# Two feed-forward layers of a streaming encoder: 16 of 22 up-projection tiles as seven block products instead of eight

## The chip, the cores and the metric

The kernel runs on one core of a Trainium2 chip, as one launch. The metric is the time of one execution on the device in microseconds. Before the change it is 1991.15 us (median of three runs, 1991.13 to 1991.19).

A core has engines that run side by side, each through its own list of instructions in order: TensorE (PE; weight loads are shown apart as PEld), VectorE (DVE), ScalarE (ACT), GpSimd (POOL) and SyncE (SP), which issues the DMAs here. TensorE reads its operands from SBUF, the on-chip memory of 128 partitions, and adds up in PSUM, which has eight banks of 512 float32 numbers per partition.

## The reference

One layer of an encoder over 512 prompt tokens and 8 x 16 sample tokens, 640 tokens together, with width 1024. It is a feed-forward part (FFN 1), a mixer of three branches (windowed attention, the gated recurrence HGRN2, and a gated linear recurrence, RG-LRU), and a second feed-forward part (FFN 2). The change is in the two feed-forward parts:

```python
D_MODEL = 1024
D_FF = 2816

def rms_norm(x, g):
    xf = x.astype(jnp.float32)
    y = xf * lax.rsqrt(jnp.mean(xf * xf, axis=-1, keepdims=True) + EPS)
    return y.astype(x.dtype) * g

def swiglu(h, w_up, w_down):
    gate, val = jnp.split(h @ w_up, 2, axis=-1)
    return (jax.nn.silu(gate) * val) @ w_down

def layer_forward(x, p, lb, cache, win_rows):
    x = x + 0.5 * swiglu(rms_norm(x, p['norm_ffn1']), p['w_ffn1_up'], p['w_ffn1_down'])
    m, st = mixer(rms_norm(x, p['norm_mix']), p, lb, cache, win_rows)
    x = x + m
    x = x + 0.5 * swiglu(rms_norm(x, p['norm_ffn2']), p['w_ffn2_up'], p['w_ffn2_down'])
    return x, st
```

All arrays are float32.

## The kernel before

**Layout.** Activations are held transposed: a block of 128 channels lies on the 128 partitions, and the 640 tokens (`T`) run along it. The 1024 channels are eight such blocks. The residual `X` has eight blocks of 640. A weight tile is 1024 x 128: eight blocks of 128 x 128 for one block of 128 outputs.

**High and low parts.** TensorE takes operands of a reduced float32 form (`F32R`). To keep the precision, every operand is split into a high part (a copy into that form) and a low part (the difference), and each product is three matmuls: high x high, high x low and low x high. `RA` and `RB` hold an activation each: eight blocks of high parts and eight of low parts.

**A projection** (`proj`, L648 to 660) loads one weight tile of 512 KB by DMA into one of three buffers `wr`, makes its high part `wh` (L654, on ScalarE or VectorE) and low part `wl` (L655, VectorE), and issues 8 blocks x 3 parts x 2 token halves = 48 matmuls of 320 columns each, into a PSUM buffer `pp` of two banks, one half of the tokens in each. There are two `pp` buffers. `scaled` (L662) moves the result out of PSUM and multiplies it by the norm's factor `RS` of each token; the gain of the norm is in `RA` or `RB` already.

**A feed-forward part** (`ffn`, L677 to 691) goes through 22 tiles of the hidden width 2816 in groups of 8, 8 and 6. For a tile, it projects the gate, applies silu (ScalarE), projects the value, multiplies the two, and splits the product into its parts in `H` (`parts`, L672). After a group it projects the group down (`w_down`) for all eight blocks of outputs and adds half of that to the residual (L689). In the last group, `done(m)` follows for each block: in FFN 1 the next norm's sums and a copy of the block to DRAM, in FFN 2 the transposes and stores of the result.

**Order of the work.** The order is made when the kernel is built. Each operation goes to a planner (`Sched`) with its reads, its writes, a duration by a small formula for its engine, and a priority. The planner lists the operations of each engine in the order in which, by these durations, they could start; among those that could start within 0.04 us it takes the one with the lowest priority number. The priority is the number of the projection (`S.item`), in program order. Three kinds of work are asked for earlier, by a lag in projections: the weight load (4), the high part (2) and the low part (1.5). Buffers with one name (a tag) are handed out in program order, and a tag that lies over the space of another waits until all of that one's buffers have been handed out and those in the way are free. On the chip each engine then runs its list in order, with semaphores for the waits.

**Space.** One array `AR` of 25600 numbers per partition holds all scratch; `arena` lays tags over it, so that FFN 1, attention, LRU, HGRN and FFN 2 use the same space one after another.

Matmuls of all kinds are issued at L394, transposes at L402; VectorE's additions and products stand at L334, its combined operation with a scalar at L348; ScalarE's functions at L358, copies at L364; DMAs at L379. The profile names lines, and most of these are the helpers' lines, so tile names (`pp`, `wr`, `wh`, `RA`) tell the groups apart.

Of the kernel before, what the change touches and what calls it, by code (L numbers as in the profile page):

```python
# [8 lines left out]
F32 = mybir.dt.float32  # L9
# [85 lines left out]
class Slot:  # L95
    __slots__ = ("ap", "lo", "hi", "free", "owner", "before")

    def __init__(self, ap, lo=None, hi=None):
        self.ap, self.lo, self.hi, self.free, self.owner, self.before = ap, lo, hi, 0.0, None, []

# [32 lines left out]
class Sched:  # L133
# [12 lines left out]
    def tag(self, name, slots, psum=False):  # L146
        for s in slots:
            for u in self.tags.values():
                v = [v for v in u.slots if s.lo is not None and v.lo is not None and v.lo < s.hi and s.lo < v.hi]
# [86 lines left out]
    def run(self):  # L236
# [13 lines left out]
        for _ in range(len(self.ops)):  # L250
# [38 lines left out]
            for b, s in zip([b for b in o.news if b.slot is None], slots):  # L289
                b.slot, b.ap, s.owner = s, s.ap, b  # L290
# [20 lines left out]
def trunk_kernel(ctx: ExitStack, tc: tile.TileContext, A: dict, O: list):  # L311
# [107 lines left out]
    DER = fixed("DER", [P, 40])  # L419
# [4 lines left out]
    NAR = 100 * 256  # L424
# [29 lines left out]
    arena(M0, [("X2", M0, 1)])
    arena(2 * M0, [("sq2", T, 1), ("acc2", T, 2), ("nh2", T, 3), ("fA2", T, 2), ("fB2", T, 2), ("yo", T, 3)])
# [134 lines left out]
    def pv(ps):  # L590
        return ps.v.r("p (a b) -> p a b", a=2)[:, :, :HT]
# [56 lines left out]
    def proj(w, r0, nk, c0, R):  # L648
# [607 lines left out]
```

## Time and profile before

| | |
|---|---|
| median of three runs | 1991.15 us |
| the profiled execution | 1991.13 us, of it 1989.3 us are the span of the profile |
| TensorE | 15086 matmuls |
| weight loads of the up-projections | 88 of 512 KB |
| VectorE, ScalarE instructions | 1922, 978 |
| granted TensorE clock, mean | 0.998 of full speed |

The time of the execution is a little more than the span: the span runs from the first to the last recorded instruction. A row of a group gives the line, the engine, the operation, the output and the inputs with their sizes, and the count; behind the bar come the busy time in us, the mean duration of one in ns, and the time that the engine stood idle just before them, with the engine and line that ended most of it. A row of the timeline gives start and duration in us; a bracket behind it is the idle time before. In the chain of waits, each piece is what held up the next.

### The profile page before, as it was taken

To read this page: it belongs to the slowest core of one execution; us is meant where nothing else is said; L and a number is where in the kernel's file an instruction comes from. 1 tells how busy PE (TensorE), PEld (TensorE's weight loads), DVE (VectorE), ACT (ScalarE), POOL (GpSimd) and SP (SyncE) were. 2 spreads that over 40 slices of the span, in tenths; PEclk is the share of its full clock that TensorE was granted. 3 is DMA by queue.
4 is the path that set the end of the run, shared out by engine and by line. 5 is a ranking of instruction groups with operands and counts; after the bars stand their busy time and mean duration, and the time that the engine had idled before them with its cause. 6 is when DMAs were issued, how large, how long until landed. Compare 5 with 4: busy or idle time off the path is not lost.

```text
span 1989.3 us, 34591 instructions
## 1 busy us (share of the span) xinstructions
PE 1959.9 (99%) x15086; PEld 1915.1 (96%) x15086; DVE 1159.4 (58%) x1922; ACT 557.3 (28%) x978; POOL 31.5 (2%) x61
## 2 busy tenths in 40 slices
PE   6999999999999999999999999999999999999998
PEld 5999999999999999999999999999999999999998
DVE  4543444456677783677557788886555443444444
ACT  5110010012468850798002333334112100110000
POOL 0000000000000000020000000000000000000000
PEclk9999999999999999999999999999999999999999
DMA  4222222224412212222322222223322222222223
GB/s 128 77 75 75 75 75 74 75 67 129 121 54 59 64 49 77 75 58 78 87 77 83 77 77 81 84 77 119 85 75 75 75 75 74 75 75 74 75 64 85
DMA packets 304434, 156.85 MB, mean 79 GB/s; under 512 B 22645, under 2 KB 301782, under 8 KB 304282
## 3 DMA queue, kind: packets, MB, share of 16 engines
q1 hardware_dynamic: 304282, 154.63, 27.0%
q8 instruction: 118, 1.93, 0.4%
q14 instruction: 34, 0.28, 0.0%
HBM read 143.32 MB, written 10.63 MB: 77 GB/s over the span
## 4 chain that ended last, share of the span: by engine, by line
PE 92%; ACT 3%; DVE 2%; SPq 1%; DMA 1%; issue 1%; DVEq 0%; ACTq 0%
PE pp L394 84%; PE me L394 4%; PE ml L394 3%; ACT L358 1%; PE ml L402 1%; ACT AR L358 1%; SPq L379 1%; PE me L402 1%; DVE AR L334 1%; DMA SK<-in_attn_sinks_dram 1%; DVE AR L348 1%; DVE RB L334 0%; DVE AR L996 0%; DMA wr<-in_w_in_dram 0%; DVE wl L655 0%
## 5 line engine op out<-in xcount | busy, mean ns | idle before, releaser
L394 PE MATMUL pp<-RA,wh 128*128 128x320 f32 x5056 | 968.1, 313 | 0.3 <-DVE RA L348 0.3
L394 PEld LDWEIGHTS pp<-RA,wh 128*128 128x128 f32 x5056 | 791.6, 189 | 10.8 <-issue 7.6
L394 PE MATMUL pp<-RA,wl 128*128 128x320 f32 x2528 | 576.7, 309 | 0.0
L394 PE MATMUL pp<-RB,wh 128*128 128x320 f32 x2880 | 539.5, 309 | 0.0
L654 DVE CAST wh<-wr 128x1024 fp32r<-128x1024 f32 (+1 forms) x221 | 151.3, 685 | 600.4 <-PE pp L394 598.8
L394 PEld LDWEIGHTS pp<-RB,wh 128*128 128x128 f32 x2880 | 452.5, 188 | 0.0
L394 PEld LDWEIGHTS pp<-RA,wl 128*128 128x128 f32 x2528 | 423.8, 188 | 0.3 <-DVE wl L655 0.2
L394 PE MATMUL pp<-RB,wl 128*128 128x320 f32 x1440 | 328.3, 309 | 0.0
L655 DVE TENSOR_TENSOR wl<-wr,wh 128x1024 fp32r<-128x1024 f32 (+1 forms) x252 | 302.5, 1200 | 0.6 <-DVE AR L334 0.4
L358 ACT ACTIVATE AR<-AR 128x640 f32<-128x640 f32 (+2 forms) x216 | 147.7, 685 | 522.3 <-DVE AR L334 503.2
L394 PEld LDWEIGHTS pp<-RB,wl 128*128 128x128 f32 x1440 | 241.2, 188 | 0.3 <-DVE wl L655 0.3
L334 DVE TENSOR_TENSOR AR<-AR 128x640 f32<-128x640 f32 (+8 forms) x380 | 198.4, 545 | 38.9 <-ACT AR L358 31.2
L334 DVE TENSOR_TENSOR AR<-pp,RS 128x640 f32<-128x640 f32 x168 | 137.5, 819 | 8.5 <-PE pp L394 8.1
L358 ACT ACT_TABLE_LOAD x97 | 124.5, 1283 | 5.8 <-DVE AR L334 3.7
L364 ACT CAST RA<-AR 128x640 fp32r<-128x640 f32 x30 | 21.8, 728 | 211.9 <-DVE AR L334 205.8
L364 ACT CAST RB<-AR 128x640 fp32r<-128x640 f32 x38 | 27.6, 726 | 177.1 <-DVE AR L334 177.1
L394 PE MATMUL ml<-AR 128*128 128x128 f32 (+6 forms) x576 | 68.3, 314 | 0.0
L394 PEld LDWEIGHTS me<-AR 128*32 128x32 f32 (+2 forms) x2016 | 50.5, 118 | 14.6 <-issue 9.5
L394 PE MATMUL me<-AR 128*32 128x16 f32 (+6 forms) x2016 | 63.9, 206 | 0.0
L364 ACT COPY AR<-me 128x512 f32<-128x512 f32 (+3 forms) x72 | 26.0, 375 | 115.5 <-PE me L402 92.2
L394 PEld LDWEIGHTS ml<-AR 128*128 128x128 f32 (+2 forms) x576 | 46.9, 151 | 11.6 <-ACT AR L364 2.6
L348 DVE SCALAR_TENSOR_TENSOR AR<-AR,PRM 64x512 f32<-64x512 f32 (+6 forms) x92 | 52.0, 582 | 0.9
(111 smaller groups left out, 894.0 us busy)
## 6 DMA issues: line engine op xcount, KB each, us to landing
wr<-in_w_ffn_up_dram SPq DMA_DIRECT2D x88, 512.0 KB
wr<-in_w_in_dram SPq DMA_DIRECT2D x84, 512.0 KB
wr<-in_w_ffn_down_dram SPq DMA_DIRECT2D x32, 512.0 KB
wr<-in_w_ffn_down_dram SPq DMA_DIRECT2D x16, 384.0 KB
wr<-in_w_attn_o_dram SPq DMA_DIRECT2D x8, 512.0 KB
AR<-in_state_hgrn_dram SPq DMA_DIRECT2D x8, 512.0 KB
wr<-in_w_lru_o_dram SPq DMA_DIRECT2D x8, 512.0 KB
out_dram<-AR SPq DMA_DIRECT2D x8, 512.0 KB
```

The lines of the kernel that those rows point to most:

```text
L334: alts = [dve(out.n, lambda: nc.vector.tensor_tensor(out(), a(), b(), op=op))]
L348: return S.op([dve(out.n, lambda: nc.vector.scalar_tensor_tensor(out(), a(), ap_of(s), b(), op0=op0, op1=op1), isinstance(s, View))], [a, ...
L358: nc.scalar.activation(out(), a(), func, bias=ap_of(bias), scale=ap_of(scale), **kw)
L364: alts = [act(out.n, lambda: nc.scalar.copy(out(), a()), 0, a), dve(out.n * (1.0 if a.in_psum else 0.5), lambda: nc.vector.tensor_copy(out ...
L379: return S.op([("SP", 0.47, lambda: nc.sync.dma_start(ap_of(out), ap_of(a)))], [a], [out], dma=v.n * 4 * v.proto.shape[0], lag=lag)
L394: nc.tensor.matmul(o(), l(), m(), start=s, stop=e)
L402: nc.tensor.transpose(o(), i(), d())
L654: S.op([act(nk * P, lambda: nc.scalar.copy(h(), r())), dve(nk * P * 0.5, lambda: nc.vector.tensor_copy(h(), r()))], [r], [h], lag=2)
L655: S.op([dve(nk * P, lambda: nc.vector.tensor_tensor(l(), r(), h().bitcast(F32), op=ALU.subtract))], [r, h], [l], lag=1.5)
```

## The change

For tiles 6 to 21 of each feed-forward part, gate and value are now made together (`pair`). The 1024 channels are cut into two halves and the 640 tokens into two halves, so the normed activations are a 2 x 2 of blocks `x11`, `x12`, `x21`, `x22`, and the weights of gate and value a 2 x 2 as well (`g1`, `g2`, `u1`, `u2`). Their block product, eight products of blocks, is done with seven by Strassen's method in Winograd's form: four sums of activation blocks (`t1` to `t4`), made once per layer (`combos` and its `rest`), four sums of weight blocks (`s1` to `s4`) in each pair, and seven additions of the results. Each product is 4 blocks x 3 parts = 12 matmuls of 320 columns into one PSUM bank.

Since the sums need the same scale for each token, the activations are normed first: `combos` multiplies `X` by gain and `RS`, and `pair` has no `RS` behind it. The first six tiles stay as they were, except that their result is moved out of PSUM half by half. The groups of tiles are now 6, 8 and 8. `combos` is issued behind tile 2; `rest` behind tile 5, since it writes over the operand of the first six tiles (`R`).

`pp` becomes four buffers of one bank each for two of two, and every reader of a projection now reads two banks in two instructions. The value weights have a buffer of their own, `vr` (one), beside the three `wr`; parts of the weight sums are in `vh` and `vl` (four each). To make room, `AR` shrinks from 25600 to 13864 numbers; three regions `RX`, `RY` and `RW` beside it change between float32 and `F32R` use from phase to phase, and a phase begins only when the one before is wholly done. The scratch tags of all stages are laid out anew.

```diff
+class Region:
+    def __init__(self, name, base, n, protos, make):
+        self.name, self.base, self.n, self.protos, self.make = name, base, n, protos, make
+        self.now, self.tiles = -1, {}
+    def tile(self, phase):
+        if phase not in self.tiles:
+            assert phase > self.now
+            self.now = phase
+            self.tiles[phase] = self.make(self.name, self.n, phase)
+        assert phase == self.now
+        return self.tiles[phase]
+    def slots(self, phase, at, n, k):
+        return [Slot(self.protos[phase][:, a:a + n], self.base + a, self.base + a + n, self, phase)
+                for a in range(at, at + n * k, n) if a + n <= self.n or 1 / 0]
 
 
...
-    for name, n, w in (("pp", 2, 1024), ("me", 2, 512), ("ml", 2, 512)):
+    for name, n, w in (("pp", 4, 512), ("me", 2, 512), ("ml", 2, 512)):
...
+    def combos_tags(sfx, ry, rx, at):
+        S.tag("vx" + sfx, RW.slots(rx - 1, 0, T, 6) + of_ar(at, T, 4))
+        S.tag("vB" + sfx, RX.slots(rx, 0, 2560, 2) + RY.slots(ry, 0, 2560, 1))
+        arena(at, [("vS" + sfx, 512, 3), ("vr" + sfx, 1024, 1)])
+        in_region(RW, rx, [("vh" + sfx, 512, 4), ("vl" + sfx, 512, 4)])
...
         S.op([dve(nk * P, lambda: nc.vector.tensor_tensor(l(), r(), h().bitcast(F32), op=ALU.subtract))], [r, h], [l], lag=1.5)
-        ps = S.buf("pp")
+        ps = [S.buf("pp") for _ in range(2)]
         for k in range(nk):
-            mm([(pv(ps)[:, i, :], a[:, k, :], R[:, o + k, i * HT:(i + 1) * HT].at(o + k), k == 0 and j == 0, k == nk - 1 and j == 2)
+            mm([(ps[i][:, :HT], a[:, k, :], R[:, o + k, i * HT:(i + 1) * HT].at(o + k), k == 0 and j == 0, k == nk - 1 and j == 2)
                 for j, (a, o) in enumerate(((wh, 0), (wh, 8), (wl, 0))) for i in range(2)])
         return ps
 
     def scaled(tag, ps, late=False):
 
         b = S.buf(tag)
+        for i, (o, p) in enumerate(halves(b.v, ps)):
+            if late:
+                cp(o, p, only=("ACT", "DVE"))
+            else:
+                tt(o, p, hv(RS.v)[:, i, :], ALU.mult)
         if late:
-            cp(hv(b.v), pv(ps), only=("ACT", "DVE"))
             tt(b.v, b.v, RS.v, ALU.mult)
-        else:
-            tt(hv(b.v), pv(ps), hv(RS.v), ALU.mult)
         return b
 
...
-    def ffn(wu, wd, R, H, sfx, done):
-        for f0, nf in ((0, 8), (8, 8), (16, 6)):
+    def combos(norm, R, sfx):
+        vs = [S.buf("vx" + sfx).v for _ in range(8)]
+        for k in range(KD):
+            h, q = k // 4, (k % 4) // 2
+            for n in range(2):
+                o = vs[(h * 2 + q) * 2 + n].r("p (a b) -> p a b", a=2)[:, k % 2, :].at(k % 2)
+                stt(o, hv(xk(k))[:, n, :], prm(norm + k), hv(RS.v)[:, n, :], ALU.mult, ALU.mult)
+        def x(h, n, q):
+            return vs[(h * 2 + q) * 2 + n]
+        def put(dst, q, v):
+            hi, lo = dst(0, q), dst(1, q)
+            cp(hi, v, only=("ACT",))
+            tt(lo, v, hi.cast(F32), ALU.subtract)
+        def in_r(j):
+            return lambda part, q: R[:, 4 * j + 2 * part + q, :].at(4 * j + 2 * part + q)
+        def in_b(b):
+            return lambda part, q: b[:, (2 * part + q) * T:(2 * part + q + 1) * T].at((part, q))
+        vb = [in_b(S.buf("vB" + sfx)) for _ in range(3)]
+        ops = {"x11": in_r(0), "x21": in_r(1), "x22": in_r(2), "t1": in_r(3), "t2": vb[0], "t3": vb[1], "t4": vb[2]}
+        for q in range(2):
+            a, b = S.buf("vx" + sfx), S.buf("vx" + sfx)
+            tt(a.v, x(1, 1, q), x(0, 1, q), ALU.subtract)
+            put(ops["t3"], q, a.v)
+            tt(b.v, x(0, 1, q), x(0, 0, q), ALU.subtract)
+            tt(b.v, x(1, 1, q), b.v, ALU.subtract)
+            put(ops["t2"], q, b.v)
+            tt(b.v, x(1, 0, q), b.v, ALU.subtract)
+            put(ops["t4"], q, b.v)
+        def rest():
+            for q in range(2):
+                put(ops["x11"], q, x(0, 0, q))
+            for name, h, n in (("x21", 1, 0), ("x22", 1, 1)):
+                for q in range(2):
+                    put(ops[name], q, x(h, n, q))
+            for q in range(2):
+                tt(x(0, 1, q), x(0, 1, q), x(0, 0, q), ALU.subtract)
+                put(ops["t1"], q, x(0, 1, q))
+        return ops, rest
+    def pair(wu, f, ops, sfx):
+        S.item += 2
+        gr, ur = S.buf("wr"), S.buf("vr" + sfx)
+        U = ur.v.r("p (k f) -> p k f", k=KD)
+        for v, c0 in ((gr.v, f * P), (U, FF + f * P)):
+            dma(v, wu[:, c0:c0 + P].rearrange("(k p) f -> p k f", p=P), lag=6)
+        def sub(out, a, b, lag, op=ALU.subtract):
+            S.op([dve(out.n, lambda: nc.vector.tensor_tensor(out(), a(), b(), op=op))], [a, b], [out], lag=lag)
+        def hi(out, a, lag):
+            S.op([act(out.n, lambda: nc.scalar.copy(out(), a()))], [a], [out], lag=lag)
+        def half(b):
+            return b.v.r("p (k f) -> p k f", k=4)
+        wh, wl = S.buf("wh"), S.buf("wl")
+        hi(wh.v, gr.v, 3.0)
+        sub(wl.v, gr.v, wh.v.cast(F32), 2.9)
+        G, g1, g2, u1, u2 = {}, gr[:, 0:4, :], gr[:, 4:8, :], U[:, 0:4, :], U[:, 4:8, :]
+        s1, s2, s3, s4 = (S.buf("vS" + sfx) for _ in range(4))
+        def parts_of(name, v, lag):
+            h, l = S.buf("vh" + sfx), S.buf("vl" + sfx)
+            H, L = half(h), half(l)
+            hi(H, v, lag)
+            sub(L, v, H.cast(F32), lag - 0.1)
+            G[name] = H, L
+        sub(half(s1), u1, u2, 2.8, ALU.add)
+        sub(half(s2), half(s1), g1, 2.75)
+        parts_of("s2", half(s2), 2.7)
+        sub(half(s3), g1, u1, 2.4)
+        parts_of("s3", half(s3), 2.35)
+        parts_of("u2", u2, 2.05)
+        parts_of("s1", half(s1), 1.7)
+        sub(half(s4), g2, half(s2), 1.4)
+        parts_of("s4", half(s4), 1.35)
+        G["g1"], G["g2"] = ((wh[:, o:o + 4, :], wl[:, o:o + 4, :]) for o in (0, 4))
+        def product(w, x):
+            (H, L), B, ps = G[w], ops[x], S.buf("pp")
+            def of(part, k):
+                return B(part, k // 2).r("p (a b) -> p a b", a=2)[:, k % 2, :]
+            for q in range(2):
+                mm([(ps[:, :HT], a[:, k, :], of(part, k), k == 0 and j == 0, k == 3 and j == 2)
+                    for k in (2 * q, 2 * q + 1) for j, (a, part) in enumerate(((H, 0), (H, 1), (L, 0)))])
+            return ps[:, :HT]
+        g, u = S.buf("fA" + sfx), S.buf("fB" + sfx)
+        (g0, g1_), (u0, u1_) = ([hv(b.v)[:, i, :].at(i) for i in range(2)] for b in (g, u))
+        cp(u0, product("g1", "x11"), only=("ACT",))
+        tt(g1_, product("s2", "t2"), u0, ALU.add)
+        tt(g0, product("g2", "x21"), u0, ALU.add)
+        fn(g0, g0, AF.Silu)
+        tt(u1_, product("s3", "t3"), g1_, ALU.add)
+        tt(u0, product("u2", "t4"), u1_, ALU.add)
+        ps = product("s1", "t1")
+        tt(u1_, ps, u1_, ALU.add)
+        tt(g1_, ps, g1_, ALU.add)
+        tt(g1_, product("s4", "x22"), g1_, ALU.add)
+        fn(g1_, g1_, AF.Silu)
+        return g, u
+    def ffn(wu, wd, norm, R, H, sfx, done, aside=()):
+        ops = None
+        for f0, nf in ((0, 6), (6, 8), (14, 8)):
             for f in range(nf):
-                late = not sfx and f0 + f < 2
-                g = scaled("fA" + sfx, proj(wu, 0, KD, (f0 + f) * P, R), late)
-                fn(g.v, g.v, AF.Silu)
-                u = scaled("fB" + sfx, proj(wu, 0, KD, FF + (f0 + f) * P, R), late)
+                for at, job in aside:
+                    if at == f0 + f:
+                        job()
+                if f0:
+                    g, u = pair(wu, f0 + f, ops, sfx)
+                else:
+                    late = not sfx and f < 2
+                    g = scaled("fA" + sfx, proj(wu, 0, KD, f * P, R), late)
+                    fn(g.v, g.v, AF.Silu)
+                    u = scaled("fB" + sfx, proj(wu, 0, KD, FF + f * P, R), late)
                 tt(u.v, g.v, u.v, ALU.mult)
                 parts(H, f, u.v)
+                if f0 + f == 2:
+                    ops, rest = combos(norm, R, sfx)
+            if f0 == 0:
+                rest()
             for m in range(KD):
                 ps = proj(wd, f0 * P, nf, m * P, H)
-                x = xk(m)
-                stt(hv(x), pv(ps), 0.5, hv(x), ALU.mult, ALU.add)
-                if f0 == 16:
+                for o, p in halves(xk(m), ps):
+                    stt(o, p, 0.5, o, ALU.mult, ALU.add)
+                if f0 == 14:
                     done(m)
 
...
-    ffn(A["w_ffn1_up"][0], A["w_ffn1_down"][0], RA, RB, "", spill)
+    ffn(A["w_ffn1_up"][0], A["w_ffn1_down"][0], G1, RA, RB, "", spill)
...
-    ffn(A["w_ffn2_up"][0], A["w_ffn2_down"][0], RB, RA, "2", finish)
+    ffn(A["w_ffn2_up"][0], A["w_ffn2_down"][0], G2, RB, RA, "2", finish)
```

More of the change, by code (lines that the diff above doesn't have):

```diff
@@ L95, with __init__, place @@
 class Slot:
-    __slots__ = ("ap", "lo", "hi", "free", "owner", "before")
-    def __init__(self, ap, lo=None, hi=None):
+    __slots__ = ("ap", "lo", "hi", "free", "owner", "before", "region", "phase")
+    def __init__(self, ap, lo=None, hi=None, region=None, phase=0):
         self.ap, self.lo, self.hi, self.free, self.owner, self.before = ap, lo, hi, 0.0, None, []
+        self.region, self.phase = region, phase
+    def place(self):
+        return self.ap if self.region is None else self.region.tile(self.phase)[:, self.lo - self.region.base:self.hi - self.region.base]
+class Region:
[12 more added lines that the diff above has]
+                for a in range(at, at + n * k, n) if a + n <= self.n or 1 / 0]
 class Tag:
@@ L148, in tag @@
             for u in self.tags.values():
-                v = [v for v in u.slots if s.lo is not None and v.lo is not None and v.lo < s.hi and s.lo < v.hi]
+                v = [v for v in u.slots if s.lo is not None and v.lo is not None and (v.lo < s.hi and s.lo < v.hi or
+                     s.region is not None and v.region is s.region and v.phase < s.phase)]
                 if v:
@@ L454, in trunk_kernel, with make @@
-    arena(M0, [("X2", M0, 1)])
-    arena(2 * M0, [("sq2", T, 1), ("acc2", T, 2), ("nh2", T, 3), ("fA2", T, 2), ("fB2", T, 2), ("yo", T, 3)])
+    R_, F_ = RA.v.r("p k t -> p (k t)")(), AR
+    types = {"RX": (F32, F32R, F32, F32R), "RY": (F32R, F32, F32R), "RW": (F32, F32R, F32, F32R)}
+    def make(name, n, phase):
+        return pool.tile([P, n], types[name][phase], tag=name, name=f"{name}{phase}")
+    RX, RY, RW = (Region(name, base, n, [R_ if t is F32R else F_ for t in types[name]], make)
+                  for name, base, n in (("RX", 100000, M0), ("RY", 200000, 4 * T), ("RW", 300000, 4096)))
@@ new lines, in in_region, with of_ar @@
+    def in_region(region, phase, tags):
+        at = 0
+        for name, n, k in tags:
+            S.tag(name, region.slots(phase, at, n, k))
+            at += n * k
+    def of_ar(at, n, k):
+        assert at + n * k <= NAR
+        return [Slot(AR[:, a:a + n], a, a + n) for a in range(at, at + n * k, n)]
+    def combos_tags(sfx, ry, rx, at):
[3 more added lines that the diff above has]
+        in_region(RW, rx, [("vh" + sfx, 512, 4), ("vl" + sfx, 512, 4)])
@@ new lines, in trunk_kernel @@
+    F0 = M0 + T + 1024 + 6 * T
+    in_region(RX, 0, [("x0", 1024, 4), ("xs", 1024, 1)])
+    arena(0, [("X1", M0, 1), ("sq", T, 1), ("pst", 1024, 1), ("fA", T, 2), ("fB", T, 2), ("acc", T, 2)])
+    combos_tags("", 0, 1, F0)
+    arena(F0, [("nh", T, 3)])
+    in_region(RX, 2, [("MG", M0, 1)])
+    in_region(RY, 1, [("gx", T, 4)])
+    in_region(RW, 2, [("qb", 1024, 2), ("pw", 1024, 2)])
+    arena(0, [("ck", 512, 1), ("kc", 1024, 1), ("vc", 512, 2), ("vd", 1280, 1),
+              ("kd", T, 4), ("pT", 1792, 1), ("sS", 512, 1), ("sT", 512, 1), ("sO", 256, 1), ("qs", 256, 2), ("ms", 512, 1),
+              ("qq", T, 2), ("qt", T, 1), ("qr", T, 1), ("qu", T, 1), ("sm", 16, 4)])
@@ L456, in trunk_kernel @@
+    in_region(RW, 2, [("mgB", T, 6)])
+    A2 = M0 + 7 * T
+    arena(0, [("X2", M0, 1)])
+    arena(M0, [("sq2", T, 1), ("acc2", T, 2), ("fA2", T, 2), ("fB2", T, 2), ("nh2", T, 3)])
+    combos_tags("2", 2, 3, A2)
+    arena(A2, [("yo", T, 3)])
     dram = ctx.enter_context(tc.tile_pool(name="dram", bufs=1, space=bass.MemoryType.DRAM))
@@ L588, in hv, with halves @@
         return v.r("p (a b) -> p a b", a=2)
-    def pv(ps):
-        return ps.v.r("p (a b) -> p a b", a=2)[:, :, :HT]
+    def halves(v, ps):
+        return [(hv(v)[:, i, :], p[:, :HT]) for i, p in enumerate(ps)]
     class Norm:
@@ L718, in gate @@
         g = mg(m) if tag is None else S.buf(tag).v
-        tt(hv(g), pv(proj(W, 0, KD, col + m * P, RA)), hv(RS.v), ALU.mult)
+        for i, (o, p) in enumerate(halves(g, proj(W, 0, KD, col + m * P, RA))):
+            tt(o, p, hv(RS.v)[:, i, :], ALU.mult)
         fn(g, g, AF.Sigmoid)
@@ L725, in merge @@
             ps = proj(wo, 0, KD, m * P, RB)
-            if gates is None:
-                tt(hv(mg(m)), pv(ps), hv(mg(m)), ALU.mult)
-            else:
-                g = gates[m]
-                tt(hv(g), pv(ps), hv(g), ALU.mult)
+            g = mg(m) if gates is None else gates[m]
+            for o, p in halves(g, ps):
+                tt(o, p, o, ALU.mult)
+            if gates is not None:
                 tt(mg(m), mg(m), g, ALU.add)
@@ L1204, in trunk_kernel @@
         x = xk(m)
-        tt(hv(x), pv(ps), hv(x), ALU.add)
+        for o, p in halves(x, ps):
+            tt(o, p, o, ALU.add)
         n2.add(m)
```

26 lines of the change are left out of this document (10 added, 16 removed).

## The prediction

> **What bounds the kernel now.** I read the page's busy times first, then the chain of waits that ended last, then the stretches of the two feed-forward layers (FFN 1 and FFN 2), then single instructions there.
>
> ```profile
> span 1989.3 us, 34591 instructions
> PE 1959.9 (99%) x15086; PEld 1915.1 (96%) x15086; DVE 1159.4 (58%) x1922; ACT 557.3 (28%) x978; POOL 31.5 (2%) x61
> PE 92%; ACT 3%; DVE 2%; SPq 1%; DMA 1%; issue 1%; DVEq 0%; ACTq 0%
> ```
>
> TensorE is busy all the time and carries 92% of the chain. A busy TensorE need not be at its peak, so the chain in order of time (start, us, what) gives its pace, and the busy times by stretch show who else works there:
>
> ```profile
> 45.82 449.68 PE pp L394 x3066
> 1521.50 424.16 PE pp L394 x2892
> 1956.98 5.28 PE pp L394 x36
> ...
> core 0: us, PE busy (x) PEld busy (x) DVE busy (x) ACT busy (x) POOL busy (x), PEclk, DMA share, GB/s
> 35.00:500.00 465.00, 465.00 (x3165) 464.77 (x3165) 224.72 (x304) 52.99 (x76) 2.47 (x5) 1.00 0.28 82
> 806.00:926.00 120.00, 114.68 (x764) 111.81 (x763) 93.06 (x167) 108.12 (x134) 12.80 (x16) 1.00 0.22 65
> 1010.00:1380.00 370.00, 370.00 (x4033) 345.04 (x4032) 282.24 (x530) 121.81 (x209) 6.42 (x17) 1.00 0.27 78
> 1500.00:1975.00 475.00, 475.00 (x3248) 474.99 (x3247) 219.86 (x268) 43.35 (x61) 0.00 (x0) 1.00 0.26 75
> ```
>
> 449.68 / 3066 and 424.16 / 2892 both give 0.1467 us per matmul of 128x128 by 320 columns, in one unbroken piece each, at a granted clock of 1.00. In both layers nothing but the number of matmuls sets the time. VectorE is busy 48% (224.72 / 465), ScalarE 11%, DMA 28%. So fewer matmuls means less time, for as long as VectorE, which gets the new work, stays under TensorE's time.
>
> **The change, part by part.**
>
> *Matmuls removed.* One tile of an up-projection is now two projections (gate and value) of 8 blocks x 3 high/low parts x 2 token halves = 96 matmuls, 96 x 0.1467 = 14.08 us. As seven block products it is 7 x 4 blocks x 3 parts = 84, 12.32 us. 12 matmuls fewer in 16 tiles of 2 layers: 384 x 0.1467 = 56.3 us. The down-projections only change how 22 tiles are grouped (6, 8, 8 for 8, 8, 6): 22 x 8 x 6 matmuls either way, no difference.
>
> Could the matmuls themselves get dearer? The old code alternates two PSUM banks; a product puts 12 matmuls in a row into one. Gate matmuls of the LRU stage do three in a row into one bank, each with other weights or another operand:
>
> ```profile
> 805.54 0.31 PE L394 MATMUL me<-NH,BH 128*128 128x320 f32 x1
> 805.69 0.31 PE L394 MATMUL me<-NL,BH 128*128 128x320 f32 x1
> 805.84 0.30 PE L394 MATMUL me<-NH,BL 128*128 128x320 f32 x1
> 805.98 0.31 PE L394 MATMUL me<-NH,BH 128*128 128x320 f32 x1
> 806.12 0.31 PE L394 MATMUL me<-NL,BH 128*128 128x320 f32 x1
> 806.27 0.31 PE L394 MATMUL me<-NH,BL 128*128 128x320 f32 x1
> ```
>
> Their starts are 0.14 to 0.15 us apart, the same pace. And the page counts as many weight loads as matmuls (15086 of each), so the shared weights of two neighbours saved no load before. I take 0.1467.
>
> *VectorE's new work in a pair (gate and value of one tile).* From the diff: the low part of the gate weights (1024 elements), four sums of weight blocks and five low parts (nine of 512), seven additions that read products from PSUM (320 each), then as before the product of gate and value and its low part (640 each): 19 instructions. Groups by form (busy, mean ns | idle before), and a piece of the timeline (start, duration):
>
> ```profile
> L655 DVE TENSOR_TENSOR wl<-wr,wh 128x1024 fp32r<-128x1024 f32 x236 | 287.3, 1217 | 0.6 <-DVE AR L334 0.4
> L334 DVE TENSOR_TENSOR AR<-pp,RS 128x640 f32<-128x640 f32 x168 | 137.5, 819 | 8.5 <-PE pp L394 8.1
> L334 DVE TENSOR_TENSOR AR<-me,AR 128x512 f32<-128x512 f32 x8 | 5.5, 690 | 0.8 <-PE me L394 0.7
> L334 DVE TENSOR_TENSOR AR<-AR 128x320 f32<-128x320 f32 x80 | 36.4, 490 | 0.2
> L348 DVE SCALAR_TENSOR_TENSOR RA<-AR,PRM,RA 128x640 fp32r<-128x640 f32 x16 | 13.8, 883 | 3.3 <-ACT RA L358 3.1
> ...
> 72.85 0.69 DVE L654 CAST wh<-wr 128x1024 fp32r<-128x1024 f32 x1 [4.48 <-PE pp L394]
> 73.46 0.82 DVE L334 TENSOR_TENSOR AR<-pp,RS 128x640 f32<-128x640 f32 x1
> 74.19 1.22 DVE L655 TENSOR_TENSOR wl<-wr,wh 128x1024 fp32r<-128x1024 f32 x1
> 75.33 0.82 DVE L334 TENSOR_TENSOR AR<-AR 128x640 f32<-128x640 f32 x1
> 76.94 0.83 DVE L334 TENSOR_TENSOR RB<-AR,RB 128x640 fp32r<-128x640 f32 x1 [0.79 <-ACT RB L364]
> ...
> 1092.25 1.68 DVE L348 SCALAR_TENSOR_TENSOR AR<-AR 128x640 f32<-128x640 f32 x2 [1.69 <-ACT AR L358]
> ```
>
> By durations the pair costs 1.22 + 9 x 0.69 + 7 x 0.49 + 2 x 0.82 = 12.50 us. But an instruction that does not need its forerunner starts before that one has ended: the one of 0.82 is followed after 0.73, the one of 1.22 after 1.14. Two that depend on each other take 1.68, the full 0.84 each. From 0.73 for 640 and 1.14 for 1024 the step is 0.41 / 384 per element; that puts 512 at 0.59 and 320 at 0.39. With these starts the pair costs 1.14 + 9 x 0.59 + 7 x 0.39 + 2 x 0.73 = 10.64 us. So VectorE needs between 10.64 and 12.50 us against TensorE's 12.32: from 86% to just over. The nearer bound is the lower one, since the sums are asked for one pair ahead and evictions stand between them, so few neighbours depend on each other; but at some 90% in strict order there will be small waits. A product holds one of four banks for 1.76 us (12 x 0.1467), so TensorE can be three products, 5.3 us, ahead of a late eviction. Bounds of the loss per pair: 0 and 12.50 - 12.32 = 0.18; I take 0.1, 3 us over 32 pairs (range 0 to 6).
>
> *ScalarE in a pair*: high parts and copies.
>
> ```profile
> L654 ACT CAST wh<-wr 128x1024 fp32r<-128x1024 f32 x31 | 32.5, 1048 | 66.5 <-PE pp L394 66.5
> L364 ACT COPY AR<-ml 128x512 f32<-128x512 f32 x37 | 21.5, 584 | 43.6 <-PE ml L394 32.9 <-PE ml L402 10.4
> L358 ACT ACTIVATE AR<-me,PRM 128x320 f32<-128x320 f32 x32 | 16.0, 525 | 61.8 <-PE me L394 61.5
> L364 ACT CAST RB<-AR 128x640 fp32r<-128x640 f32 x38 | 27.6, 726 | 177.1 <-DVE AR L334 177.1
> ```
>
> 1.05 + 5 x 0.58 + 3 x 0.53 + 0.73 = 6.3 of 12.32 us, half. Nothing on the path.
>
> *The operand blocks, once per layer.* Per layer VectorE norms 16 halves (320 elements; the 640 form with a scalar is 0.88, half the elements about 0.55), then 8 sums and 14 low parts of 640 at 0.82: 8.8 + 18.0 = 27 us. Of these 8.8 + 11.5 come during tiles 2 to 5, where VectorE leaves half of 4 x 14.08 us idle, 28 us; the other ten (8.2 us) overwrite the projection's operand, so they start with the down-projections of the first six tiles, 8 x 5.28 = 42 us, of which VectorE needs there about 2.5 us of each 5.28. All of it lies beside TensorE; I cost it at 0. With that cover gone it would be 54 us for both layers, nearly the whole gain. What is late next: buffers of the first pair's sums reuse the space of the normed halves, so its load and its sums wait until the last ten are through: 10 x 0.82 + 0.73 = 9 us, then a load (3.5 us, below), then 3 us of sums, 16 of the 42 us.
>
> *The value weights' one buffer (`vr`).* Gate weights rotate through three `wr` buffers; a value block can be loaded only after the low part of `u2` of the pair before has been taken. SP issues in order, so gate loads stand behind that wait.
>
> ```profile
> 841.76 3.54 DMA wr<-in_w_in_dram
> SPq L379 <- DVE wl L655: 1405.2, 219, 17.5
> ```
>
> A load is seen on the chain once, 3.54 us; SP's waits today are nearly all for a weight buffer, and TensorE does not notice. The cycle of `vr` is the load, 0.4 for the issue, and six VectorE steps with one ScalarE step, 6 x 0.69 + 0.58 = 4.7: 8.6 of 12.32 us. Cost 0, 3.7 us to spare.
>
> *The rest.* Evictions of all other projections become two of 320 for one of 640: 2 x 0.39 - 0.73 = 0.05 us of VectorE each, where it is 76% busy at most (282.24 / 370, in the HGRN stage): 0. Silu runs on halves: inside ScalarE's slack. The moved scratch areas and the finer banks give the planner another order in the mixer. TensorE is idle there for 5.3 us in the LRU stage (120 - 114.68), so I bound this by 5 us either way and take 0.
>
> *Sum.* The profiled execution took 1991.13 us (span 1989.3 and 1.83 outside it), the median of the runs is 1991.15. 1991.1 - 56.3 + 3 = **1938 us**, and 1930 to 1946 with the two bounds (0 to 6, and 5 either way).
>
> **The rivals.**
>
> 1. *VectorE becomes the bound in the pairs.* For it: 12.50 by full durations exceeds 12.32 already, and a low part can wait for its high part, as the row at 76.94 did for 0.79. Against it: the overlapping starts, and that there are 19 instructions of two pairs to choose from. It decides from 12.32 us a pair. One such wait in each pair makes 13.3; between 12.50 and 13.3 I take 12.9: 1934.8 + 0.58 x 32 = **1953 us** (1941 to 1966). [...]
>
> 2. *The mixer loses by the new order.* Place: the LRU stage, where TensorE already waits for chains through ScalarE (108.12 of 120 us busy). If these waits treble, 10 us go: **1948 us**. Against it: the same areas were shared between the same stages before.
>
> 3. *Slower: the single `vr` buffer sets the pace.* If each of the six VectorE steps of its cycle is served behind one other instruction (0.6 to 1.2 us), the cycle is 8.6 + 6 x 1.1 = 15.2 us, and TensorE waits in every pair. It decides from 12.32, and eats the gain from 14.08, that is when the cycle is 5.5 us longer than worked out: 1991.1 + (15.2 - 14.08) x 32 = **2027 us**. For it: an engine that is 90% busy serves few things at once. Against it: the prep of a pair is asked for early and would have to be late at every step.
>
> 4. *The change does not do what it says*: fewer matmuls, but each dearer in a single bank. 1991 us if a matmul took 0.168; the six rows at 805.54 all but exclude it.
>
> **How the numbers follow.** Forecast 0.65; rival 1 0.18; rival 2 0.08; rival 3 0.07; rival 4 0.02. The forecast alone spans 1930 to 1946; rival 1 up to two thirds of its span and rival 2 lie below 1962, so 1930 to 1962 leaves out rivals 3 and 4 and the top of rival 1, together under 0.2. A change within 0.2% (4 us) can't be told from none. Faster: 0.65 + 0.18 + 0.08 = 0.91; the same 0.02; slower 0.07.
>
> **What would show it.** The chain inside the two layers should show matmuls on `pp` at 0.1467 each, with 384 fewer in all (14702); a pair should take 12.3 to 12.5 us. VectorE should be busy some 10.6 to 12.5 us per pair without TensorE's waits naming it. If idle time before matmuls is put down to VectorE's sums or to low parts of `vh`/`vl`, it is rival 1; if SP waits for the low part of `u2` and VectorE for the load of `vr`, rival 3; if the stretch between the layers grows beyond 1000 us, rival 2. The prediction is wrong if pairs take over 12.8 us, or if a piece of the operand blocks shows up on the chain.

## The result

The changed kernel takes 1942.23 us (median of four runs, 1941.57 to 1942.27), against 1991.17 us for the kernel before. The ratio is 0.9752, with a 95% interval of 0.9741 to 0.9764. The prediction was 1938 us, and 1930 to 1962.

The page of the changed kernel, busy times and chain:

```profile
span 1940.5 us, 35075 instructions
PE 1907.8 (98%) x14702; PEld 1862.7 (96%) x14702; DVE 1359.5 (70%) x2531; ACT 743.8 (38%) x1278; POOL 25.3 (1%) x58
PE 93%; DVE 3%; ACT 2%; SPq 1%; DMA 1%; issue 0%; DVEq 0%; ACTq 0%
```

There are 14702 matmuls, 384 fewer, and VectorE has gone from 58% to 70%. TensorE still carries the chain.

To divide the 48.8 us that the span lost, I use a mark that both kernels have: the small matmuls that sum the squares for a norm (`NH` by `ones`). The first of them stands just behind the end of FFN 1, the last just behind the start of FFN 2. The row of that tile gives both times (count, duration in ns, first to last start). It is from the kernel before, then from the changed one:

```profile
L394 PE MATMUL me<-NH,ones x20: 307/308/308, 503.2 to 1521.0; 128*128 128x320 f32 x20
```

```profile
L419 PE MATMUL me<-NH,ones x20: 304/310/311, 476.3 to 1500.5; 128*128 128x320 f32 x20
```

| stretch | before | after | difference |
|---|---|---|---|
| to the first mark (FFN 1) | 503.2 | 476.3 | -26.9 us |
| between the marks (mixer) | 1017.8 | 1024.2 | +6.4 us |
| behind the last mark (FFN 2) | 468.3 | 440.0 | -28.3 us |

The marks lie a little behind the seams: the next stage has had 48 matmuls by then in the kernel before, and 54 in the changed one. By the first matmul of the mixer (496.05 and 468.37 us) and of FFN 2 (1513.72 and 1492.33) the differences are -27.7, +6.3 and -27.4 us. So the two layers gave 55.1 to 55.2 of the 56.3 us worked out for their pairs. Of what is lacking, 0.9 us is one wait of TensorE for an eviction on VectorE at the start of FFN 2 (at 1508.04), which is gone in the kernel with the evictions together (below). The mixer, whose arithmetic the change leaves alone, lost 6.4.

Inside the pairs, TensorE waits for nothing. The products with `t2` and `t3` read `RX`, in turn, and their rows in TensorE's timeline of the changed kernel show the pace (start, duration):

```profile
172.69 1.93 PE L419 MATMUL pp<-RX,RW 128*128 128x320 f32 x12
177.97 1.92 PE L419 MATMUL pp<-RX,RW 128*128 128x320 f32 x12
185.01 1.93 PE L419 MATMUL pp<-RX,RW 128*128 128x320 f32 x12
190.29 1.92 PE L419 MATMUL pp<-RX,RW 128*128 128x320 f32 x12
197.33 1.93 PE L419 MATMUL pp<-RX,RW 128*128 128x320 f32 x12
```

The starts with `t2`, 172.69, 185.01 and 197.33, are 12.32 us apart. The busy times in a stretch of five pairs of the changed kernel, with 5 x 19 instructions of VectorE, show how much VectorE has left:

```profile
core 0: us, PE busy (x) PEld busy (x) DVE busy (x) ACT busy (x) POOL busy (x), PEclk, DMA share, GB/s
172.69:234.29 61.60, 61.60 (x423) 61.60 (x421) 55.17 (x95) 30.63 (x50) 0.00 (x0) 1.00 0.29 82
```

55.17 / 5 is 11.0 us of VectorE a pair, 90% of 12.32. ScalarE is at 50%.

The mixer's loss lies in the LRU stage. These are the waits of TensorE there (us in total, times, longest), in the changed kernel from 839 to 922 us, and then in the same stretch of the kernel before, from 865 to 945 us:

```profile
PE pp L419 <- DVE AR L359: 3.6, 1, 3.6
PE me L419 <- ACT NH L389: 2.4, 1, 2.4
PE me L419 <- DVE NL L359: 0.8, 1, 0.8
PE pp L419 <- DVE wl L718: 0.6, 1, 0.6
```

```profile
PE me L394 <- ACT AR L358: 1.9, 4, 0.7
PE me L394 <- DVE NL L334: 1.8, 2, 0.9
PE me L394 <- ACT NH L364: 1.2, 2, 0.6
```

They come to 7.4 us after and 4.9 us before, and the longest grew from 0.9 to 3.6 us.

The timeline of VectorE in the changed kernel shows where the 3.6 us come from (start, duration), with the waiting matmul last:

```profile
838.09 0.48 DVE L359 TENSOR_TENSOR AR<-pp,RS 128x320 f32<-128x320 f32 x1
...
839.89 1.48 DVE L1188 TENSOR_TENSOR_SCAN AR<-AR 128x640 f32<-128x640 f32 x1
...
842.67 0.99 DVE L373 SCALAR_TENSOR_TENSOR AR<-RY,PRM,AR 128x112 f32<-128x112 f32 x2
843.58 0.82 DVE L359 TENSOR_TENSOR RB<-AR,RB 128x640 fp32r<-128x640 f32 x1
...
846.82 0.48 DVE L359 TENSOR_TENSOR AR<-pp,RS 128x320 f32<-128x320 f32 x1
...
847.36 0.71 PE L419 MATMUL pp<-RA,wh 128*128 128x320 f32 x3 [3.62 <-DVE AR L359]
```

At 838.09 VectorE takes a projection's first bank. The next instruction on `pp` stands 8.7 us later in its list, behind the scan (839.89) and pieces of the convolution of the LRU (842.67). It takes the second bank. TensorE needs that second bank from 843.7 on, and gets it at 847.36. Before, one instruction of 640 (0.82 us on the mean) freed both banks at once.

The waits are not the whole loss. The granted clock (the third number from the end) in short stretches of the changed kernel:

```profile
840.00:850.00 10.00, 5.82 (x34) 5.07 (x33) 10.00 (x20) 4.88 (x6) 1.31 (x2) 0.95 0.04 9
850.00:856.00 6.00, 6.00 (x36) 6.00 (x35) 2.30 (x5) 5.93 (x8) 0.00 (x0) 0.80 0.58 171
856.00:880.00 24.00, 23.95 (x163) 23.69 (x162) 19.27 (x37) 19.21 (x25) 2.13 (x3) 1.00 0.17 47
880.00:886.00 6.00, 2.82 (x18) 2.32 (x17) 6.00 (x16) 4.07 (x5) 1.04 (x2) 1.00 0.00 0
886.00:890.00 4.00, 4.00 (x19) 4.00 (x19) 3.79 (x7) 3.94 (x6) 0.00 (x0) 0.57 0.44 129
```

Behind the two waits the clock is 0.95, 0.80 and 0.57: 10 x 0.05 + 6 x 0.20 + 4 x 0.43 = 3.4 us of matmul time lost at a clock below full. With the 2.5 us by which the waits grew that is 5.9 of the 6.4 us that the mixer lost.

### The profile page after: what moved, and what is told of

It reads as the page before. It is cut to its first block, busy times and chain, and to the rows that moved or that the text cites. A ratio compares the mean times of both kernels' runs of the same rounds, so it can differ in the third digit from the quotient of the medians.

```text
span 1940.5 us, 35075 instructions
## 1 busy us (share of the span) xinstructions
PE 1907.8 (98%) x14702; PEld 1862.7 (96%) x14702; DVE 1359.5 (70%) x2531; ACT 743.8 (38%) x1278; POOL 25.3 (1%) x58
## 4 chain that ended last, share of the span: by engine, by line
PE 93%; DVE 3%; ACT 2%; SPq 1%; DMA 1%; issue 0%; DVEq 0%; ACTq 0%
PE pp L419 84%; PE me L419 4%; PE ml L419 3%; PE ml L427 1%; SPq L404 1%; PE me L427 1%; ACT L383 1%; DVE AR L373 1%; ACT AR L383 1%; DMA SK<-in_attn_sinks_dram 1%; DVE AR L359 1%; DVE wl L718 0%; DVE AR L1188 0%; DVE RB L359 0%; DVE wh L717 0%
## 5 line engine op out<-in xcount | busy, mean ns | idle before, releaser
L419 PE MATMUL pp<-RA,wh 128*128 128x320 f32 x4288 | 837.1, 315 | 4.2 <-DVE AR L359 3.9
L419 PEld LDWEIGHTS pp<-RA,wh 128*128 128x128 f32 x4288 | 674.8, 189 | 15.3 <-issue 7.6
L419 PE MATMUL pp<-RB,wh 128*128 128x320 f32 x2112 | 404.9, 309 | 1.4 <-DVE AR L359 0.9
L419 PEld LDWEIGHTS pp<-RB,wh 128*128 128x128 f32 x2112 | 333.9, 188 | 2.2 <-DVE AR L359 1.4
L359 DVE TENSOR_TENSOR AR<-AR 128x640 f32<-128x640 f32 (+10 forms) x271 | 143.5, 534 | 27.1 <-ACT AR L383 20.6
L383 ACT ACTIVATE AR<-AR 128x640 f32<-128x640 f32 (+3 forms) x180 | 110.4, 614 | 85.0 <-DVE AR L359 76.9
L359 DVE TENSOR_TENSOR AR<-pp,AR 128x320 f32<-128x320 f32 x240 | 113.6, 485 | 22.3 <-PE pp L419 20.2
L419 PE MATMUL pp<-RX,RW 128*128 128x320 f32 x768 | 123.2, 309 | 0.0
L419 PEld LDWEIGHTS pp<-RX,RW 128*128 128x128 f32 x768 | 115.2, 188 | 0.0
L800 DVE TENSOR_TENSOR RW<-AR,RW 128x512 fp32r<-128x512 f32 x160 | 108.8, 685 | 1.0
```

What stands on the lines that cost most here:

```text
L359: alts = [dve(out.n, lambda: nc.vector.tensor_tensor(out(), a(), b(), op=op))]
L383: nc.scalar.activation(out(), a(), func, bias=ap_of(bias), scale=ap_of(scale), **kw)
L419: nc.tensor.matmul(o(), l(), m(), start=s, stop=e)
L800: S.op([dve(out.n, lambda: nc.vector.tensor_tensor(out(), a(), b(), op=op))], [a, b], [out], lag=lag)
```

## The experiments

The questions were: what of the change costs the mixer its time, by which way, and how much room VectorE, the operand blocks and the buffer `vr` really have.

### The layout and the banks without the products

The edit leaves every up-projection tile to two projections, and keeps all else of the changed kernel.

```diff
-                if f0:
+                if False:
                     g, u = pair(wu, f0 + f, ops, sfx)
...
-                if f0 + f == 2:
-                    ops, rest = combos(norm, R, sfx)
-            if f0 == 0:
-                rest()
```

> The changed kernel without the block products: all 22 tiles by two projections each, in groups of 6, 8 and 8, with the new scratch layout and the four one-bank buffers. Theory P (the pairs gained 54.5 us and the new layout or the new banks cost the mixer 6.4 us): 1997 to 1998 us, with 1024 us between the sums of the two norms where it was 1017.6 before. Rival Q (the mixer loses because of what the pairs leave behind in the order of the work): 1991 us, and 1017.6 us between the norms.

Measured: 1998.32 us (1997.38 to 1998.52), 1.0035 times the kernel before (1.0022 to 1.0048). Between the marks lie 1528.5 - 503.2 = 1025.3 us. Theory P holds: the loss comes without any pair. This kernel and the changed one differ by the products and their operand blocks alone, and their times by 1998.3 - 1942.2 = 56.1 us, against 56.3 worked out.

### The banks alone

The edit takes the kernel before and gives it four `pp` buffers of one bank and two evictions of 320.

```diff
-    for name, n, w in (("pp", 2, 1024), ("me", 2, 512), ("ml", 2, 512)):
+    for name, n, w in (("pp", 4, 512), ("me", 2, 512), ("ml", 2, 512)):
...
+        for i, (o, p) in enumerate(halves(b.v, ps)):
+            if late:
+                cp(o, p, only=("ACT", "DVE"))
+            else:
+                tt(o, p, hv(RS.v)[:, i, :], ALU.mult)
...
-            tt(hv(b.v), pv(ps), hv(RS.v), ALU.mult)
```

> The kernel before with one edit: four one-bank buffers and two evictions of 320 in place of two two-bank buffers and one eviction of 640. If the banks cost the mixer its 6.4 us: 1997 to 1998 us. If the scratch layout does: 1991 us. If each does a part: between.

Measured: 1998.29 us (1997.45 to 1998.63), 1.0034 times before (1.0021 to 1.0046). The marks stand 1024.8 us apart, and the waits of the LRU stage are those of the changed kernel:

```profile
PE pp L394 <- DVE AR L334: 3.6, 1, 3.6
PE me L394 <- ACT NH L364: 2.4, 1, 2.4
```

All of the mixer's loss comes with the banks and their two evictions; the new scratch layout costs nothing that shows.

### VectorE with more to do in each pair

Two experiments add subtractions of 512 elements, whose result nothing reads.

```diff
+        J = S.buf("vJ" + sfx)
+        for lag in (2.6, 1.9):
+            sub(half(J), g1, g2, lag)
         sub(half(s1), u1, u2, 2.8, ALU.add)
```

> The changed kernel with two more VectorE subtractions of 512 elements in every pair, into a scratch tile that nothing reads. Theory S (what an instruction costs VectorE is the distance between starts): 10.64 + 2 x 0.59 = 11.8 us a pair, still under TensorE's 12.32, so 1942 to 1944 us. Rival D (it costs its whole duration): 12.50 + 2 x 0.69 = 13.9 us a pair, 1.4 to 1.6 more than TensorE, so 1990 us or so.

Measured: 1942.48 us, unchanged. In five pairs VectorE is busy for 59.38 of 61.60 us, 11.9 us a pair, where theory S had 11.8. Rival D is out: what an instruction costs VectorE here is not its whole duration; by full durations, this run would have come to some 1990 us. The prediction's rows show the same: there an instruction starts 0.73 us after the start of one with a duration of 0.82. Even if a group of pairs hides half of such a loss, as the next run shows, rival D would have cost some 20 us here.

> The same with five more subtractions in every pair. Theory S: 10.64 + 5 x 0.59 = 13.6 us a pair, 1.3 over TensorE's 12.32 in 32 pairs: 1942 + 41 = 1983 us, with TensorE's waits put down to VectorE. Rival D: 12.50 + 5 x 0.69 = 15.95 us a pair, 1942 + 116 = 2058 us.

Measured: 1962.81 us, half of the loss that theory S expected, and far from D's. The timeline of TensorE in this kernel shows why. In FFN 1's first group of pairs it begins to wait at the end of the fourth pair, which starts its product with `t2` at 196.78. The last row is the granted clock around the wait of 1.83 us:

```profile
196.78 1.93 PE L419 MATMUL pp<-RX,RW 128*128 128x320 f32 x12
204.21 3.78 PE L419 MATMUL pp<-RA,RW 128*128 128x320 f32 x24 [0.22 <-DVE AR L359]
209.59 1.93 PE L419 MATMUL pp<-RX,RW 128*128 128x320 f32 x12
218.64 5.33 PE L419 MATMUL pp<-RA,RW 128*128 128x320 f32 x24 [1.83 <-DVE AR L359]
...
247.56 3.79 PE L419 MATMUL pp<-RA,RW 128*128 128x320 f32 x24 [1.83 <-DVE AR L359]
252.94 1.93 PE L419 MATMUL pp<-RX,RW 128*128 128x320 f32 x12
...
218.00:224.00 6.00, 5.36 (x26) 5.36 (x27) 5.07 (x11) 1.18 (x3) 0.00 (x0) 0.72 0.01 3
```

From 196.78 to 252.94 four pairs take 56.16 us, 14.0 each. Of that, 5.33 - 3.78 = 1.55 us went because the 24 matmuls at 218.64 ran partly at a lower clock; without it the pairs are 13.65 us apart, and theory S had 13.6. So its price of an instruction holds, and what it had wrong is how many pairs pay. The pairs before that stand 12.3 apart: TensorE waits for the first time in the fourth pair, and in the second group, where VectorE is as much too slow, only in the seventh. I put this down to work made ahead, with the down-projections in between to catch up in (VectorE is busy for 42.5 of the 64 us from 266 to 330); no run varied it. So in this kernel an overload of VectorE in a group of eight pairs is paid only in the later ones.

### Two-bank buffers, shared by two products

```diff
-    for name, n, w in (("pp", 4, 512), ("me", 2, 512), ("ml", 2, 512)):
+    for name, n, w in (("pp", 2, 1024), ("me", 2, 512), ("ml", 2, 512)):
...
-            (H, L), B, ps = G[w], ops[x], S.buf("pp")
+            if not banks:
+                b = S.buf("pp")
+                banks.extend(pv(b)[:, i, :].at(i) for i in range(2))
+            (H, L), B, ps = G[w], ops[x], banks.pop(0)
```

> The changed kernel with the old two-bank buffers: one eviction of 640 for each projection again, and in a pair two products share one buffer, a bank each. Theory B (in the LRU stage the two evictions of one projection stand far apart in VectorE's list, the second bank comes free 3.6 us late, TensorE waits, and after the wait its granted clock is 0.5 for 3.4 us): the mixer's loss goes, 1936 us, no wait of 3.6 us and no drop of the clock in the LRU stage. Rival V (a pair needs its banks freed one by one): the mixer gains 6 us, but the pairs come more than 12.32 us apart, and the time stays at 1942 us or above.

Measured: 2012.03 us (2011.86 to 2012.31), 1.0102 times before (1.0087 to 1.0117): slower than without the products. Both statements are right in part. Between the marks lie 1527.1 - 509.1 = 1018.0 us: the mixer's loss is gone, and so is the wait of 3.6 us. One drop of the clock is still there, which theory B did not expect (0.83 from 910 to 920 us, behind two short waits; more on it in the last section). But the pairs pay for it. TensorE in this kernel, with one copy of ScalarE:

```profile
160.51 1.04 PE L419 MATMUL pp<-RX,RW 128*128 128x320 f32 x6
161.58 0.43 ACT L389 COPY AR<-pp 128x320 f32<-128x320 f32 x1 [1.88 <-PE pp L419]
162.06 1.14 PE L419 MATMUL pp<-RX,RW 128*128 128x320 f32 x6 [0.52 <-ACT AR L389]
166.42 1.14 PE L419 MATMUL pp<-RY,RW 128*128 128x320 f32 x6 [0.58 <-DVE AR L359]
170.78 2.91 PE L419 MATMUL pp<-RA,RW 128*128 128x320 f32 x18 [0.58 <-DVE AR L359]
175.28 1.04 PE L419 MATMUL pp<-RX,RW 128*128 128x320 f32 x6
```

Three waits of 0.5 to 0.6 us in a pair, and 175.28 - 160.51 = 14.8 us to the next one (14.4 on the mean of seven). The matmul at 162.06, halfway through the pair's second product, waits for ScalarE's copy of the first product, which began at 161.58 and reads the other bank of the same buffer. The copy itself had stood idle until the six matmuls at 160.51 were done, though they write the bank that it does not read. So in this kernel two products that share a buffer of two banks wait for each other, which is most of the loss: (14.4 - 12.3) x 32 = 67 of the 76 us by which this kernel misses 1936. Whether the chip needs these waits, or only the tracking of who uses a buffer, no run here tells. With one buffer for each bank the pairs run at 12.32.

### Four banks, and the two evictions kept together

The edit hands the planner the two evictions of a projection as one operation of VectorE, so that they stand next to each other; the down-projections' two additions to the residual likewise. The buffers stay at one bank each.

```diff
+    def both(out, ps, b, op):
+        def emit():
+            for i, p in enumerate(ps):
+                nc.vector.tensor_tensor(hv(out)[:, i, :](), p[:, :HT](), hv(b)[:, i, :](), op=op)
+        S.op([("DVE", 2 * (0.066 + 1.042e-3 * HT), emit)], [ps[0].v, ps[1].v, b], [out])
...
-                tt(o, p, hv(RS.v)[:, i, :], ALU.mult)
...
+            both(b.v, ps, RS.v, ALU.mult)
```

> The changed kernel with its four one-bank buffers, where the planner gets the two evictions of a projection as one operation, so that they stand next to each other in VectorE's list (the first copies of FFN 1, which are made before the norm's factor is known, stay apart). Theory B (their distance costs the time): 1936 us. Rival C (that there are two instructions for one costs it): 1942 us.

Measured: 1933.25 us (1932.98 to 1934.52), 0.9709 times before (0.9692 to 0.9725). It has the marks 1491.6 - 475.0 = 1016.6 us apart, and the pairs as before 12.32. No wait of TensorE between the marks is over 2.2 us, and the clock stays at 1.00 where it fell. The evictions of this kernel stand in pairs, and a stretch across the same part of the LRU stage shows it:

```profile
841.53 0.87 DVE L655 TENSOR_TENSOR AR<-pp,RS 128x320 f32<-128x320 f32 x2
845.33 0.88 DVE L655 TENSOR_TENSOR AR<-pp,RS 128x320 f32<-128x320 f32 x2
...
835.00:845.00 10.00, 8.73 (x58) 8.30 (x58) 10.00 (x21) 6.36 (x8) 1.06 (x2) 1.00 0.13 36
845.00:855.00 10.00, 9.66 (x66) 9.34 (x65) 4.86 (x12) 9.88 (x12) 0.00 (x0) 1.00 0.36 105
```

Theory B holds, rival C falls: there are still two instructions for one.

To see it apart from the products, the same edit was made on the kernel with the banks alone.

> The kernel before with four one-bank buffers and two evictions for one, which the planner gets as one operation, so that they stand next to each other. Theory B (the distance between the two evictions in VectorE's list cost 7 us in the kernel with the banks alone): 1990 to 1992 us, and a granted clock of 1.00 through the LRU stage. If the one-bank buffers or the second instruction cost it: 1998 us.

Measured: 1990.91 us, 0.9997 times before (0.9987 to 1.0007). The 7 us of the banks alone are gone, and the clock is at 1.00 from 840 to 930 us.

Last, the changed kernel and the one with the evictions together, next to each other on one chip.

> The changed kernel once more, beside the next one on the same chip: 1942 us.

> The changed kernel with the two evictions of a projection as one operation of the planner, once more: 1933 us, 9 us under the changed kernel.

Measured: 1941.03 us (1940.79 to 1942.34) and 1932.67 us (1932.51 to 1933.42). The second is 8.4 us faster, and beats both kernels: 0.9705 times the kernel before (0.969 to 0.9719). The mixer has 7.2 of the 8.4 (1023.8 and 1016.6 us between the marks); the rest is spread over the two layers.

### The operand blocks made twice

```diff
-                stt(o, hv(xk(k))[:, n, :], prm(norm + k), hv(RS.v)[:, n, :], ALU.mult, ALU.mult)
+                for _ in range(2):
+                    stt(o, hv(xk(k))[:, n, :], prm(norm + k), hv(RS.v)[:, n, :], ALU.mult, ALU.mult)
...
-            cp(hi, v, only=("ACT",))
-            tt(lo, v, hi.cast(F32), ALU.subtract)
+            for _ in range(2):
+                cp(hi, v, only=("ACT",))
+                tt(lo, v, hi.cast(F32), ALU.subtract)
```

> The changed kernel with the operand blocks' norming, high parts and low parts all made twice: 8.8 + 11.5 = 20 us more of VectorE in each layer and 10 us more of ScalarE. If this work lies beside TensorE, as predicted: 1942 to 1944 us. If some of it is on the path: up to 1942 + 41 = 1983 us.

Measured: 1956.21 us, 14 us more. In FFN 1 the pairs start 6.6 us later and then run at their 12.32; the loss is ahead of them, at the first down-projections:

```profile
122.50 0.82 DVE L359 TENSOR_TENSOR RA<-RW,RA 128x640 fp32r<-128x640 f32 x1
123.24 0.82 DVE L359 TENSOR_TENSOR RA<-AR,RA 128x640 fp32r<-128x640 f32 x1
...
126.18 0.95 DVE L718 TENSOR_TENSOR wl<-wr,wh 128x768 fp32r<-128x768 f32 x1
127.19 0.56 PE L419 MATMUL pp<-RB,wl 128*128 128x320 f32 x2 [3.10 <-DVE wl L718]
```

The low parts of the activation blocks (into `RA`) stand in VectorE's list ahead of the low part of the second down-projection's weights (`wl`), and TensorE waits for the latter. Behind the wait of 3.10 us the clock is 0.72 from 127 to 133 us, another 1.7 us. The work made once fits; a second copy does not.

### The value weights loaded twice

```diff
-            dma(v, wu[:, c0:c0 + P].rearrange("(k p) f -> p k f", p=P), lag=6)
+            for _ in range(2 if c0 >= FF else 1):
+                dma(v, wu[:, c0:c0 + P].rearrange("(k p) f -> p k f", p=P), lag=6)
```

> The changed kernel with the value weights of every pair loaded twice, one load after the other, into the one buffer. By the prediction's working the cycle of that buffer is 8.6 us and becomes 8.6 + 3.5 = 12.1, still under the pair's 12.32: 1942 to 1946 us. If the buffer sets the pace already or has little to spare: up to 3.5 us more in each of 32 pairs, 2050 us.

Measured: 1960.16 us, 18 us more. In FFN 1's first group, TensorE waits from the fifth pair on, in each pair, for the parts of a weight sum (`RW`):

```profile
209.34 0.56 PE L419 MATMUL pp<-RX,RW 128*128 128x320 f32 x2
210.21 1.74 PE L419 MATMUL pp<-RX,RW 128*128 128x320 f32 x10 [0.31 <-DVE RW L801]
222.47 0.55 PE L419 MATMUL pp<-RX,RW 128*128 128x320 f32 x2
223.35 1.74 PE L419 MATMUL pp<-RX,RW 128*128 128x320 f32 x10 [0.32 <-DVE RW L801]
```

The pairs are 222.47 - 209.34 = 13.1 us apart. If the buffer `vr` sets this pace, its cycle with two loads is 13.1 us, where 12.1 was expected. If the second load adds the 3.5 us seen on the chain, one load has a cycle of 9.6, and 2.7 us to spare. That it adds just that was not measured. In the changed kernel VectorE waits for the load of `vr` too (seven times in FFN 1 from 160 to 450 us, 1.1 us at the longest), and SP for low parts of weight blocks: the signs that the prediction named for rival 3 are there, but no wait reaches TensorE.

## Why the prediction was right, and where it was not

*The matmuls.* Right in number and price: 384 fewer, 0.1467 us each in a single bank too, pairs at 12.32 us. The layers gained 55.2 us of 56.3.

*VectorE in the pairs.* The step gave 10.64 to 12.50 us and took 3 us of loss. The loss was nil: TensorE waits for nothing in the pairs, and VectorE is busy 11.0 us of each. The lower bound was the right one to choose: the time with two more subtractions is unchanged, and with five more, where VectorE sets the pace, the pairs came 13.65 us apart where 10.64 + 5 x 0.59 gives 13.6. For the loss, though, the step treated each pair by itself. The run with five more shows that in a group of eight TensorE gets through three to six pairs before it waits.

*The operand blocks.* Costed at 0, and that is right to 0.5 us in FFN 1, all that the 27.7 us to the first matmul of the mixer lack of 28.2. The step counted eight sums where `combos` and `rest` have ten, so a layer's blocks cost VectorE 28.5 us by its prices and not 27, which changes nothing in the forecast. The size of the cover was wrong: 42 us of down-projections were named, but in strict order the blocks hide only until VectorE must make the second down-projection's low weights. Made twice, they cost 14 us instead of the 0 expected.

*The one buffer `vr`.* Also 0, and also with less room than worked out: pairs 13.1 us apart with two loads, where a cycle of 12.1 was expected.

*"The rest": two evictions for one at 0.* This is the step that failed. It priced the second instruction, 0.05 us of VectorE, and asked if VectorE has room. It did say that the finer banks give the planner another order in the mixer, and bounded that by 5 us either way, because TensorE is idle for 5.3 us in the LRU stage. That idle time limits what a better order can win, not what a worse one can lose, and the 6.4 us lie outside the bound. What the step did not ask is where the planner puts the second instruction. The planner orders by earliest start, so once an eviction is two operations, other work that is ready comes between them, and a bank is given back late. That cost 6.4 us, in waits and in the clock behind them. Rival 2 named the right place (the LRU stage), the new order and a like size (10 us), but another way (ScalarE's waits trebled), and it argued about the scratch areas alone; the runs show that these cost nothing and the banks all of it. Its sign, a stretch between the layers of over 1000 us, could tell nothing: between the marks it was 1017.8 us before the change.

*The sum.* 1938 forecast, 1942.2 measured: 3 us too many in the pairs, and 6.4 too few in the mixer. That these two offset each other in part is luck. The size of the gain came out because its main term rested on rows of the same matmuls; the miss is in the term that was taken as 0.

## What to carry to other kernels

Where an order is planned by start times, an operation cut in two is no longer one place in the list: ask what can come between the halves, and who waits for the second; keep them together if the next work needs what both of them free. A price of nothing should name not only an idle engine but the next thing in that engine's strict order. And before a matmul count is cut, add a little work to the engine that gets the new load: here two and five more instructions showed where its room ends.

## What the runs showed of the hardware

A wait of TensorE can cost 1.7 us more than its length. In the five places that are read here the granted clock fell behind a wait, and each time the row of the clock gives the same loss: 1.7 us in each of the two places of the changed kernel shown above (10 x 0.05 + 6 x 0.20, and 4 x 0.43), 6 x 0.28 = 1.7 with five more subtractions and with the blocks made twice, and 10 x 0.17 = 1.7 with the two-bank buffers. In short stretches of the changed kernel, the clock is 0.95 from 848.50 to 849.00 us, 0.50 from 849.00 to 852.00 and 0.63 from 852.00 to 852.50, which makes 0.05 + 3.0 + 0.37 = 3.4 us at 0.50. At the second place it is 0.75, 0.50, 0.50 and 0.54 in the four us from 886 to 890: 0.5 + 2.0 + 0.92 = 3.4 us again.

In these runs the length of a wait does not tell whether the clock falls. It fell behind waits of 3.62 us, of 3.10, of 2.38 and 0.81 close to each other, of 1.83, and, with the two-bank buffers, of 0.63 and 0.90:

```profile
911.94 0.42 PE L419 MATMUL me<-NH,BH 128*128 128x320 f32 x1 [0.63 <-ACT NH L389]
913.25 0.42 PE L419 MATMUL me<-NL,BH 128*128 128x320 f32 x1 [0.90 <-DVE NL L359]
...
910.00:920.00 10.00, 8.47 (x45) 7.98 (x45) 7.65 (x15) 8.73 (x9) 0.00 (x0) 0.83 0.33 96
```

It stayed at 1.00 behind almost the same two waits in the kernel before (0.60 and 0.90, at 906 and 907 us), behind the second wait of 1.83 in the run with five more subtractions (its 24 matmuls took 3.79 us, not 5.33), and behind 2.2 us with the evictions together. What decides is open.

In the kernel with two-bank buffers, the first product of a pair could not share a buffer with the second without a wait of 0.5 to 0.6 us, although the two use different banks; whether that is the chip or the program's tracking is open. And VectorE's instructions overlap enough that nineteen of them, 12.5 us by their durations, keep it busy for only 11.0 us of a 12.32 us pair.
